# Two expert numbers taken early: the first head's two best experts computed straight from its top keys

## The chip, the cores and the metric

The kernel runs on one core of one Trainium2 chip. The metric is the device time of one execution in microseconds (us); lower is better. Its matrix products run on TensorE (PE in the profile, its weight loads PEld), element-wise work on VectorE (DVE), ScalarE (ACT) and GpSimd (POOL); SyncE (SP) issues most of the weight transfers, and POOL issues the indirect ones.

## The reference, cut to what matters

Two transformer blocks follow one another on 256 tokens of width 1024. The first ends in a layer of experts chosen per token (`peer_ffn`), and the change lies in it:

```
q = (xb @ w_query).reshape(tb, 8, 2, 128)
s = einsum('thpd,hpnd->thpn', q, sub_keys)            # 8 heads, 2 halves, 128 keys each
top_s, top_i = top_k(s, 16)                           # the 16 best keys of each half
cand_s = top_s[:, :, 0, :, None] + top_s[:, :, 1, None, :]
cand_i = top_i[:, :, 0, :, None] * 128 + top_i[:, :, 1, None, :]
best_s, pos = top_k(cand_s, 16)                       # the 16 best sums of the 256 pairs
eid = take_along_axis(cand_i, pos)                    # 16 expert numbers per head
gate = softmax(best_s)
act = gelu(einsum('thkd,td->thk', expert_down[eid], xb))
out = einsum('thkd,thk->td', expert_up[eid], gate * act)
```

An expert number is the key of the first half times 128, plus the key of the second half. `top_k` gives values in falling order, so the best pair of a head is always (best key of half 0, best key of half 1), and the second best pair is one of (best, second) and (second, best).

## The kernel before

The 256 tokens are two tiles of 128 (t = 0 and 1), a token on each partition. Each token has 8 heads x 16 slots = 128 experts, so that there are 256 fetches: one per tile and slot. A fetch (`fetch`, the indirect transfer at L764) reads for each of 128 tokens one row of 2048 floats of `uv` (the expert's down vector and its up vector side by side) into a buffer `uv`. It is issued by POOL, which first needs the expert numbers in `eid`. Each fetch is then used in four steps: VectorE multiplies the down half with the normed token `xn` and sums (`junk`, L768); ScalarE applies Gelu and the gate (L770, L771) and builds a diagonal matrix `dg` from the 128 weights (L773); TensorE multiplies `dg` with the up half and accumulates in PSUM (L775, two products of 512 columns, each shown as two instructions). The buffer is free again after the last of these. There are seven `uv` buffers at first (`uvs = [up] * 7`), and nine after the query weights are done and their memory is given back.

The expert numbers come from `queries` (the query projection, in pieces of weights that SP loads as `raw`, ScalarE rounds to `wh` at L178, VectorE turns into the remainder `wl` at L179, and TensorE multiplies three times at L184 to L186), the scores `sS` (L643, L644), `extract` (the 16 best of a row: the best eight at L607, their places at L610, their removal at L613, the next eight at L616, their places at L619) and `choose` (80 candidate sums, `extract` once more on these, and the look-up that ends in `eid` at L689 and the gates at L697). `picks` strings these together for a group of heads as a generator; `picking` takes steps from it, up to a credit of time or to the end of a group.

The order at the start of the stage, as the program is written: the query projection of the first two pieces and the scores of head 0 for both tiles; `picking(1e6, 0, 1)`, all of head 0's extraction and choice for tile 0; then, queued behind the write of `eid` on VectorE, the product of `xn` with the tokens (L800) and the next piece of `queries`; then the loop over the fetches of tile 0, in which after each slot come some steps of later heads' picks, and after every few slots one more piece of the query projection, each queued behind that slot's product on VectorE and its diagonal on ScalarE (`behind`). After the last query piece (slot 59) the loop goes on with pieces of the memory's key and value projection in the query's place. The second tile's 128 fetches follow, and then the second block.

The program is built by a layer that places the semaphores itself and fixes each engine's queue before the run: it takes instructions in the order in which they are written, and where one would still wait by its own cost figures, it may put a later one that is ready in front. So a small instruction can stand a little before or behind its place in the text.

Of the kernel before, what the change touches and what calls it, by code (L numbers as in the profile page):

```python
# [14 lines left out]
U32 = mybir.dt.uint32  # L15
AF = mybir.ActivationFunctionType
OP = mybir.AluOpType
# [108 lines left out]
class K:  # L126
# [573 lines left out]
    def experts(self):  # L700
# [3 lines left out]
        nc, I = self.nc, self.I  # L704
        with self.tc.tile_pool(name="p2", bufs=1, reuse_waits="tile") as p2, \
                self.tc.tile_pool(name="up", bufs=1, reuse_waits="tile") as up:
            def P(shape, tag, dt=F32, bufs=1):
                return p2.tile([128] + shape, dt, name=tag, tag=tag, bufs=bufs)
# [6 lines left out]
            sS = [[P([2, 128], f"sS{t}{h}") for h in range(8)] for t in range(2)]  # L715
            vals = [P([16, 16], f"vals{t}") for t in range(2)]
            idx = [P([16, 16], f"idx{t}", U32) for t in range(2)]
            self.gate = [P([8, 16], f"gate{t}") for t in range(2)]
            self.eid = [P([8, 16], f"eid{t}", U32) for t in range(2)]
            mr = [P([2, 128], f"mr{i}") for i in range(2)]  # L720
            xn = [P([1024], "xn0"), None]

            def picks(t, h0, H):
                for h in range(h0, h0 + H):
                    yield from self.extract([sS[t][h][:, i] for i in range(2)], [mr[h % 2][:, i] for i in range(2)],
                                            [vals[t][:, 2 * h + i] for i in range(2)],
                                            [idx[t][:, 2 * h + i] for i in range(2)], 410)
                yield from self.choose(t, h0, H, vals, idx, P)

            units = [(0, h, 1) for h in range(4)] + [(0, 4, 2), (0, 6, 2)] + [(1, h, 2) for h in (0, 2, 4, 6)]  # L730
            pick = [(u, picks(*u)) for u in units]
            debt = [0]

# [22 lines left out]
            def fetch(t, acc):  # L756

                gates = self.gate[t].rearrange("p h k -> p (h k)")
                eids = self.eid[t].rearrange("p h k -> p (h k)")
                for s in range(128):  # L760
                    pool = uvs[count[0] % len(uvs)]
                    count[0] += 1
                    x = pool.tile([128, 2048], F32, name="uv", tag="uv", bufs=uvs.count(pool))
                    nc.gpsimd.indirect_dma_start(x, None, I["uv"],  # L764
                                                 bass.IndirectOffsetOnAxis(ap=eids[:, s:s + 1], axis=0))
                    w = up.tile([128, 1], F32, name="dots", tag="dots", bufs=6)
                    junk = self.junk([128, 1024], "junk", BF)
                    self.dot = nc.vector.scalar_tensor_tensor(junk, x[:, :1024], 1.0, xn[t], op0=OP.mult, op1=OP.mult,  # L768
                                                              accum_out=w)
                    nc.scalar.activation(w, w, AF.Gelu, scale=self.r[:, t:t + 1])  # L770
                    nc.scalar.activation(w, w, AF.Copy, scale=gates[:, s:s + 1])  # L771
                    dg = up.tile([128, 128], F32, name="dg", tag="dg", bufs=4)
                    self.diag = nc.scalar.activation(dg, self.ident, AF.Copy, scale=w)  # L773
                    for d in range(2):
                        nc.tensor.matmul(acc[d], dg, x[:, 1024 + 512 * d:1536 + 512 * d], start=s == 0, stop=s == 127)  # L775
                    yield s
# [11 lines left out]
            with self.tc.tile_pool(name="qp", bufs=1, reuse_waits="tile") as qp:  # L788
                skT = qp.tile([128, 16, 128], F32, name="skT")
                nc.gpsimd.dma_start(skT[:, 0:4], I["skT"][:, 0:4])  # L790
                query = Filler(self.queries(qp, skT, sS))
                query(2)
                with self.tc.issue_after(self.raw.ins):
                    nc.sync.dma_start(xn[0], I["ffn_gr"].to_broadcast([128, 1024]))
                    nc.sync.dma_start(skT[:, 4:16], I["skT"][:, 4:16])
                query(1)
                n = 4
                picking(1e6, 0, 1)
                with self.tc.issue_after(self.chosen.ins):
                    nc.vector.tensor_mul(xn[0], xn[0], self.xr[:, 0])  # L800
                    query(1)
                acc = two()
                tile0 = fetch(0, acc)
                for s in tile0:
                    with behind():
                        if s in (3, 7, 11) or s > 11 and s % 6 == 5:
                            query(1)
                            n += 1
                        picking(750, 0, min(8, (n + 1) // 2))
                        if s in due:  # L810
                            picking(1e6, *due[s])
                    if n >= 15:
                        break
                query.rest()
            self.qraw_cm.__exit__(None, None, None)
            with self.tc.tile_pool(name="up2", bufs=1, reuse_waits="tile") as up2:
# [19 lines left out]
                for s in fetch(1, acc):  # L836
                    with behind():
                        if s in (4, 10):
                            self.joined(0, s // 10, acc0[s // 10], gg, nc.vector)
                        if s > 10:  # L840
                            picking(750, 1, 8)
                        if s in due:
                            picking(1e6, 1, due[s])
                        if s % 6 == 2 and 10 < s < 100:
                            self.memory(1)
                        if s == 100:
                            self.memory.rest()
                        if s == 112:
                            ws = [self.piece(I["w_latq"][k], [2, 432]) for k in range(3)]
                    if s == 120:  # L850
                        A = [self.pa([128, 512]) for _ in range(2)]
                        self.latents(ws, 0, A[0])
# [860 lines left out]
```

## Time and profile before

| what | value |
|---|---|
| median of 3 runs | 1310.26 us (1310.0 to 1311.74) |
| the profiled execution: its own time | 1309.71 us |
| its span in the trace | 1307.9 us |
| granted TensorE clock, mean | 0.987 of full speed |
| busy: PE, DVE, ACT, POOL | 89%, 72%, 55%, 24% of the span |
| moved by DMA | 388.63 MB, 297 GB/s over the span |
| of it by POOL's indirect fetches (queue q0) | 268.72 MB |

The shares are means over stages with different limits: the stage of the fetches runs from about 145 us to 840 us, and the second block fills the rest. Times in the trace are counted from the start of the span. The profiled execution took 1.8 us more than its span.

### The profile page before, as it was taken

Reading aid. Unit: us, or ns where it says so; the run is one execution under the profiler, and the core shown is the slowest. Engines: PE = TensorE matmul, PEld = TensorE weight load, DVE = VectorE, ACT = ScalarE, POOL = GpSimd, SP = SyncE. Lnnn points to the kernel's source line nnn. Section 1 sums busy time; section 2 is a strip of 40 time slices with the busy share of each in tenths; the row PEclk is TensorE's granted clock in tenths of the full one; section 3 lists DMA queues with packets and bytes.
Section 4 is the critical chain, followed back from the end, with each engine's and each line's share of the span. In section 5 each row is a group of like instructions: output and inputs, shape, how many; then the busy total and the mean of one; then the engine's idle time right before and its main releaser. Section 6 shows DMA issues by size and latency. Waiting matters only on the chain. (4 is left out here: it accounts for less than half of the span.)

```text
span 1307.9 us, 16937 instructions
## 1 busy us (share of the span) xinstructions
PE 1170.6 (89%) x5430; PEld 788.3 (60%) x5430; DVE 942.7 (72%) x2252; ACT 715.9 (55%) x1627; POOL 319.3 (24%) x274
## 2 busy tenths in 40 slices
PE   7999799998879888888887778799999999999996
PEld 5787554444324343344442223389987898999995
DVE  5878687675998886555554445588977886988887
ACT  6676456453555445543443444558787565655554
POOL 0000344454445444344443333110000000000001
PEclk9999899999999999999999999999999999999998
DMA  7835699999999999999999999355424464566562
GB/s 269 284 129 170 247 419 420 420 420 401 422 421 417 420 419 421 420 421 420 421 420 421 421 421 419 160 181 164 132 97 145 135 221 142 183 185 186 188 184 96
DMA packets 82203, 388.63 MB, mean 297 GB/s; under 512 B 8244, under 2 KB 10372, under 8 KB 49348
## 3 DMA queue, kind: packets, MB, share of 16 engines
q0 software_dynamic: 36976, 268.72, 49.5%
q1 hardware_dynamic: 43124, 116.22, 27.3%
q10 hardware_dynamic: 2016, 2.62, 0.5%
q8 instruction: 43, 0.70, 0.2%
q14 instruction: 44, 0.36, 0.1%
HBM read 384.38 MB, written 3.15 MB: 296 GB/s over the span
## 5 line engine op out<-in xcount | busy, mean ns | idle before, releaser
L775 PE MATMUL pb<-uv,dg 128*128 128x512 f32 x1024 | 496.1, 618 | 104.7 <-ACT dg L773 103.8
L768 DVE SCALAR_TENSOR_TENSOR junk<-uv,xn 128x1024 bf16<-128x1024 f32 x256 | 312.5, 1221 | 177.1 <-DMA uv<-in_uv_dram,eid 173.6
L775 PEld LDWEIGHTS pb<-uv,dg 128*128 128x128 f32 x1024 | 181.8, 192 | 389.5 <-ACT dg L773 247.4
L764 POOL DMA_INDIRECT uv<-in_uv_dram,eid x256 | 302.0, 1180 | 405.8 <-PE pb L775 245.4
L179 DVE TENSOR_TENSOR wl<-raw,wh 128x1024 fp32r<-128x1024 f32 (+3 forms) x203 | 246.9, 1220 | 104.6 <-ACT wh L178 103.4
L178 ACT ACTIVATE wh<-raw 128x1024 fp32r<-128x1024 f32 (+3 forms) x203 | 211.1, 1044 | 149.3 <-PE pa L186 32.3
L770 ACT ACTIVATE dots<-dots,rs_y 128x1 f32<-128x1 f32 x256 | 75.2, 294 | 336.1 <-DVE junk L768 335.5
L185 PE MATMUL pb<-nTl,wh 128*128 128x256 f32 x416 | 117.9, 284 | 0.0
L184 PE MATMUL pb<-nTh,wh 128*128 128x256 f32 x416 | 117.7, 283 | 0.0
L186 PE MATMUL pb<-nTh,wl 128*128 128x256 f32 x416 | 117.5, 283 | 0.0
L773 ACT ACTIVATE dg<-cvt,dots 128x128 f32<-128x128 f32 x256 | 102.7, 401 | 14.0 <-DVE memkv L944 6.2
L1564 POOL TENSOR_TENSOR xs<-xr,ng 128x512 f32<-128x512 f32 x4 | 5.0, 1280 | 313.2 <-DVE xr L1562 313.2
L185 PEld LDWEIGHTS pb<-nTl,wh 128*128 128x128 f32 x416 | 79.6, 192 | 0.8
L184 PEld LDWEIGHTS pb<-nTh,wh 128*128 128x128 f32 x416 | 79.6, 192 | 0.8
L771 ACT ACTIVATE dots<-dots,gate 128x1 f32<-128x1 f32 x256 | 75.3, 294 | 8.5 <-ACT dots L770 0.4
L186 PEld LDWEIGHTS pb<-nTh,wl 128*128 128x128 f32 x416 | 79.6, 192 | 0.0
L184 PE MATMUL pa<-nTh,wh 128*128 128x256 f32 x256 | 79.1, 309 | 0.0
L186 PE MATMUL pa<-nTh,wl 128*128 128x256 f32 x256 | 74.2, 290 | 5.3 <-DVE wl L179 5.3
L185 PE MATMUL pa<-nTl,wh 128*128 128x256 f32 x256 | 72.9, 285 | 0.0
L184 PE MATMUL pa<-wh,nTh 128*128 128x512 f32 (+1 forms) x144 | 58.1, 412 | 8.6 <-ACT wh L178 8.0
L185 PE MATMUL pa<-wl,nTh 128*128 128x512 f32 (+1 forms) x144 | 57.5, 400 | 2.4 <-DVE wl L179 2.4
L186 PE MATMUL pa<-wh,nTl 128*128 128x512 f32 (+1 forms) x144 | 56.6, 393 | 0.0
(458 smaller groups left out, 1885.1 us busy)
## 6 DMA issues: line engine op xcount, KB each, us to landing
raw<-in_w_ffn_up_dram SPq DMA_DIRECT2D x44, 512.0 KB, 3.7
raw<-in_w_out_dram SPq DMA_DIRECT2D x24, 512.0 KB, 3.7
raw<-in_w_in_dram SPq DMA_DIRECT2D x23, 512.0 KB, 4.5
raw<-in_w_ffn_down_dram SPq DMA_DIRECT2D x22, 512.0 KB, 3.6
raw<-in_w_query_dram SPq DMA_DIRECT2D x16, 512.0 KB, 7.0
raw<-in_w_xbc_dram SPq DMA_DIRECT2D x16, 512.0 KB, 4.0
raw<-in_w_mem_v_dram SPq DMA_DIRECT2D x8, 512.0 KB, 10.3
uv<-in_uv_dram,eid POOLq DMA_INDIRECT x256, 17.6
```

What stands on the lines that cost most here:

```text
L178: nc.scalar.activation(h[:, s], raw[:, s], AF.Copy)
L179: self.wl = nc.vector.tensor_sub(lo[:, s], raw[:, s], h[:, s])
L184: mm(out, a[0], b[0], start=start, stop=False)
L185: mm(out, a[0], b[1], start=False, stop=False)
L186: mm(out, a[1], b[0], start=False, stop=stop)
L764: nc.gpsimd.indirect_dma_start(x, None, I["uv"], bass.IndirectOffsetOnAxis(ap=eids[:, s:s + 1], axis=0))
L768: self.dot = nc.vector.scalar_tensor_tensor(junk, x[:, :1024], 1.0, xn[t], op0=OP.mult, op1=OP.mult, accum_out=w)
L770: nc.scalar.activation(w, w, AF.Gelu, scale=self.r[:, t:t + 1])
L771: nc.scalar.activation(w, w, AF.Copy, scale=gates[:, s:s + 1])
L773: self.diag = nc.scalar.activation(dg, self.ident, AF.Copy, scale=w)
L775: nc.tensor.matmul(acc[d], dg, x[:, 1024 + 512 * d:1536 + 512 * d], start=s == 0, stop=s == 127)
L1564: nc.gpsimd.tensor_mul(xs[:, c], xr[:, t, c], g[:, c])
```

## The change

In the extraction of tile 0's head 0, after its second step (the best eight keys of both halves and their places are known) a new function `firsts` is called. With nine VectorE instructions on one or two columns it computes the head's two best expert numbers into a tile of their own, `first`: the best is the pair of the two best keys; for the second it compares the sum (best, second) with (second, best). The rest of the extraction and the whole choice stay as they are and still write all 16 numbers to `eid`. The fetches of slots 0 and 1 of tile 0 read their expert numbers from `first` and no longer from `eid`. Nothing else is edited.

```diff
@@ -720,11 +720,33 @@
+            first = P([2], "first", U32)
+
+            def firsts():
+                v, ix = vals[0], idx[0]
+                nc.vector.scalar_tensor_tensor(first[:, 0:1], ix[:, 0, 0:1], 128.0, ix[:, 1, 0:1],
+                                               op0=OP.mult, op1=OP.add)
+                s, d, f = P([2], "firsts"), P([2], "firstd"), P([2, 2], "firstf")
+                nc.vector.tensor_copy(f, ix[:, 0:2, 0:2])
+                nc.vector.tensor_add(s[:, 0:1], v[:, 0, 0:1], v[:, 1, 1:2])
+                nc.vector.scalar_tensor_tensor(s[:, 1:2], v[:, 0, 1:2], v[:, 1, 0:1], s[:, 0:1],
+                                               op0=OP.add, op1=OP.is_gt)
+                nc.vector.tensor_scalar(s[:, 0:1], s[:, 1:2], -1.0, 1.0, op0=OP.mult, op1=OP.add)
+                nc.vector.tensor_sub(d, f[:, :, 1], f[:, :, 0])
+                nc.vector.scalar_tensor_tensor(d[:, 0:1], d[:, 0:1], s[:, 1:2], f[:, 0, 0:1], op0=OP.mult, op1=OP.add)
+                nc.vector.scalar_tensor_tensor(d[:, 1:2], d[:, 1:2], s[:, 0:1], f[:, 1, 0:1], op0=OP.mult, op1=OP.add)
+                nc.vector.scalar_tensor_tensor(first[:, 1:2], d[:, 0:1], 128.0, d[:, 1:2], op0=OP.mult, op1=OP.add)
+
             def picks(t, h0, H):
                 for h in range(h0, h0 + H):
-                    yield from self.extract(...)
+                    for n, cost in enumerate(self.extract(...)):
+                        if (t, h, n) == (0, 0, 1):
+                            firsts()
+                        yield cost
@@ -762,7 +784,8 @@
-                                                 bass.IndirectOffsetOnAxis(ap=eids[:, s:s + 1], axis=0))
+                                                 bass.IndirectOffsetOnAxis(
+                                                     ap=(first if t == 0 and s < 2 else eids)[:, s:s + 1], axis=0))
```

## Rows read from the trace of the kernel before

**Rows 1.** The page's span in 40 slices: DMA share in tenths, GB/s moved.
```profile
DMA  7835699999999999999999999355424464566562
GB/s 269 284 129 170 247 419 420 420 420 401 422 421 417 420 419 421 420 421 420 421 420 421 421 421 419 160 181 164 132 97 145 135 221 142 183 185 186 188 184 96
```

**Rows 2.** Stretches of 2 us: length, PE, PEld, DVE, ACT, POOL busy, clock, DMA share, GB/s.
```profile
138.00:140.00 2.00, 2.00 (x19) 2.00 (x18) 1.89 (x15) 1.03 (x2) 0.00 (x0) 1.00 0.01 4
...
144.00:146.00 2.00, 0.00 (x0) 0.00 (x0) 2.00 (x3) 0.00 (x0) 0.98 (x1) 0.50 0.00 0
146.00:148.00 2.00, 1.54 (x7) 1.54 (x8) 0.40 (x1) 0.00 (x0) 1.39 (x3) 0.50 0.57 123
148.00:150.00 2.00, 2.00 (x11) 2.00 (x11) 0.00 (x0) 0.00 (x0) 1.63 (x2) 0.50 0.95 391
```

**Rows 3.** A stretch of 20 us, the same columns.
```profile
160.00:180.00 20.00, 17.78 (x78) 10.59 (x77) 16.97 (x59) 11.69 (x28) 8.64 (x7) 1.00 1.01 419
```

**Rows 4.** Timeline of VectorE, head 0's picks: start, length, instruction.
```profile
136.26 0.28 DVE L610 FIND_INDEX8 idx<-vals,sS 128x8 uint32<-128x128 f32 x1
...
140.40 0.17 DVE L671 SCALAR_TENSOR_TENSOR ru<-rf 128x16 f32<-128x16 f32 x1
140.49 0.17 DVE L672 SCALAR_TENSOR_TENSOR ru<-rf 128x16 f32<-128x16 f32 x1
140.69 0.19 DVE L673 TENSOR_TENSOR rab<-rg,ru 128x32 f16<-128x32 f32 x1
...
143.96 0.17 DVE L689 SCALAR_TENSOR_TENSOR eid<-rij 128x16 uint32<-128x16 f32 x1
...
145.19 1.22 DVE L179 TENSOR_TENSOR wl<-raw,wh 128x1024 fp32r<-128x1024 f32 x1
```

**Rows 5.** Timeline of POOL: the fetches' issue; in brackets idle before, releaser.
```profile
145.02 1.15 POOL L764 DMA_INDIRECT uv<-in_uv_dram,eid  x1 [34.29 <-DVE eid L689]
146.47 0.97 POOL L764 DMA_INDIRECT uv<-in_uv_dram,eid  x1 [0.30 <-issue]
...
157.41 1.76 POOL L764 DMA_INDIRECT uv<-in_uv_dram,eid  x1 [3.18 <-PE pb L775]
...
182.69 1.87 POOL L764 DMA_INDIRECT uv<-in_uv_dram,eid  x1 [4.39 <-DVE best L607]
...
315.16 1.68 POOL L764 DMA_INDIRECT uv<-in_uv_dram,eid  x1 [5.29 <-DVE wl L179]
```

**Rows 6.** Timeline of VectorE: products with fetched rows, slots 0, 3, 4, 16, last two.
```profile
150.95 1.23 DVE L768 SCALAR_TENSOR_TENSOR junk<-uv,xn 128x1024 bf16<-128x1024 f32 x1 [4.55 <-DMA uv<-in_uv_dram,eid]
...
159.68 1.23 DVE L768 SCALAR_TENSOR_TENSOR junk<-uv,xn 128x1024 bf16<-128x1024 f32 x1 [0.51 <-DMA uv<-in_uv_dram,eid]
...
164.12 1.22 DVE L768 SCALAR_TENSOR_TENSOR junk<-uv,xn 128x1024 bf16<-128x1024 f32 x1
...
196.79 1.23 DVE L768 SCALAR_TENSOR_TENSOR junk<-uv,xn 128x1024 bf16<-128x1024 f32 x1 [0.20 <-DMA uv<-in_uv_dram,eid]
...
834.95 1.22 DVE L768 SCALAR_TENSOR_TENSOR junk<-uv,xn 128x1024 bf16<-128x1024 f32 x1 [1.25 <-DMA uv<-in_uv_dram,eid]
837.43 1.23 DVE L768 SCALAR_TENSOR_TENSOR junk<-uv,xn 128x1024 bf16<-128x1024 f32 x1 [1.25 <-DMA uv<-in_uv_dram,eid]
```

**Rows 7.** Instructions on tile junk: what VectorE waited for (us, times).
```profile
  DMA uv<-in_uv_dram,eid: 173.6, 120
```

**Rows 8.** Timeline of TensorE at the start of the fetches.
```profile
146.46 0.58 PE L186 MATMUL pa<-nTh,wl 128*128 128x256 f32 x1 [5.28 <-DVE wl L179]
...
153.46 5.54 PE L775 MATMUL pb<-uv,dg 128*128 128x512 f32 x8 [2.48 <-ACT dg L773]
...
162.06 1.98 PE L775 MATMUL pb<-uv,dg 128*128 128x512 f32 x4 [0.57 <-ACT dg L773]
```

**Rows 9.** Stretches of 2 us where the query's memory is given back, columns of Rows 2.
```profile
316.00:318.00 2.00, 2.00 (x17) 1.88 (x16) 0.95 (x8) 1.11 (x4) 1.70 (x2) 1.00 0.92 328
318.00:320.00 2.00, 2.00 (x8) 0.82 (x6) 0.00 (x0) 1.11 (x3) 1.39 (x3) 1.00 0.90 340
```

More of the change, by code (lines that the diff above doesn't have):

```diff
@@ L721, in experts @@
             xn = [P([1024], "xn0"), None]
+            first = P([2], "first", U32)
[13 more added lines that the diff above has]
+                nc.vector.scalar_tensor_tensor(first[:, 1:2], d[:, 0:1], 128.0, d[:, 1:2], op0=OP.mult, op1=OP.add)
             def picks(t, h0, H):
                 for h in range(h0, h0 + H):
-                    yield from self.extract([sS[t][h][:, i] for i in range(2)], [mr[h % 2][:, i] for i in range(2)],
-                                            [vals[t][:, 2 * h + i] for i in range(2)],
-                                            [idx[t][:, 2 * h + i] for i in range(2)], 410)
+                    for n, cost in enumerate(self.extract(
+                            [sS[t][h][:, i] for i in range(2)], [mr[h % 2][:, i] for i in range(2)],
+                            [vals[t][:, 2 * h + i] for i in range(2)], [idx[t][:, 2 * h + i] for i in range(2)], 410)):
+                        if (t, h, n) == (0, 0, 1):
+                            firsts()
+                        yield cost
                 yield from self.choose(t, h0, H, vals, idx, P)
```

## The prediction, written before the run

> **What bounds the kernel now.** Start with the span in slices [rows 1]. From the sixth slice to the twenty-fifth (about 163 to 817 us) the DMA row is all nines and the rate stands at 419 to 422 GB/s in nearly every slice. No other stage looks like that: before it the rate is 129 to 284, after it below 225. So half of the kernel is a transfer stage at a steady rate, and in such a stage time is bytes over rate. One fetch is 128 rows of 8 KB, 1.05 MB: at 420 GB/s 2.50 us. The products with fetched rows agree: at the end of the stage they start 2.48 us apart, each after a wait of 1.25 us for its DMA [rows 6], and over the stage 120 of 256 products waited for a fetch, 173.6 us in all [rows 7].
>
> Then look at where the stage begins [rows 2]. From 138 to 146 us the DMA engines move next to nothing (0.01 to 0.00 of their time, four stretches), then 0.57, then 0.95 and full from there on. VectorE is full in the empty stretch (1.89 and 2.00 of 2.00): it runs head 0's extraction and choice. POOL stands until the numbers are there: its first fetch starts at 145.02 after 34.29 us of idling, released by `eid` [rows 5], which VectorE wrote from 143.96 to 144.13 [rows 4], so 0.89 us from the end of the write to the issue. The DMA engines have 1.1 us of work (0.57 of 2.00) in 146 to 148, so data begin to flow at about 146.9, 1.9 us after the issue.
>
> The chain is therefore: scores of head 0, picks on VectorE, first fetch, then bytes at 420 GB/s to the last fetch, whose product starts at 837.43 [rows 6], and behind it the second block. What moves the end of the bytes moves the whole rest.
>
> **What the change adds.** Nine small VectorE instructions between the places of the best eight (done at 136.54, [rows 4]) and the first removal. The trace has neighbours of that kind: L671 and L672, independent, start 0.09 us apart although each lasts 0.17; L673, which needs L672's result, starts 0.20 after it [rows 4]. Four of the nine need the result of the one just before (the comparison, its complement, the first blended key, the last sum), five do not: 4 x 0.20 + 5 x 0.09 = 1.25 us. Bounds: 9 x 0.09 = 0.8 if the planner fills the waits with removals that are ready, 9 x 0.20 = 1.8 if every one waits. I take 1.1, between the written order and the filled one. VectorE has no gap there [rows 2], so `eid`, and with it the third fetch, `xn` and the next weight split (at 145.19) come 1.1 us later. Waiting behind that split are TensorE's query products at 146.46, which stood 5.28 us for it [rows 8]; they now stand about 6.4.
>
> A rule speaks for a higher price. The Trainium skill, VectorE: DVE Perf Modes, section "The DRAIN you can't avoid", says that the next operation does not start until the pipe is empty, except where it is not held. By that each of the nine would cost its whole length; the same page's section "The TRN2 errata" gives (N+151)/0.96 ns for a float addition, an estimate of 0.16 us each, 1.4 us in all and a gain 0.3 us smaller than mine. The trace shows starts 0.09 us apart, so here it is the exception that holds for independent ones [rows 4].
>
> **What the change moves.** The issue of fetches 0 and 1, and their 2 x 2.50 us of data. `first` is complete 1.3 us after 136.54 in written order, at about 137.9; with four removals or searches of 0.28 us (the length in [rows 4]) put between, 138.9. Then 0.89 us to the issue: fetch 0 starts between 138.8 and 139.8, fetch 1 1.45 later (145.02 to 146.47, [rows 5]). Data flow from 140.7 at the earliest or 141.7 at the latest, for 5.0 us: done by 145.7 or 146.7. The third fetch is issued at 145.02 + 1.1 = 146.1 and its data start at 148.0. So both fetches fit whole into the empty stretch, with at least 1.3 us to spare; a slower issue (1.87 us is one of the long ones, [rows 5]) would still fit. Credit: 5.0 us of transfer leaves the saturated stage. No transfer is added and no queue of SP's is passed.
>
> The Trainium skill, DMA: Bandwidth & Descriptors, section "Where 436 GB/s comes from", says that from HBM the limit is about 358 GB/s. By that a fetch would take 2.93 us and the credit would be an estimated 5.9. The trace moves 419 to 422 for hundreds of us [rows 1], so the measurement decides.
>
> **The sum.** The saturated stage starts 1.1 us later and holds 5.0 us less: -3.9 us. On the profiled execution: 1309.71 - 3.9 = 1305.8. The median of the runs is 0.55 above that execution, so the forecast is 1310.26 - 3.9 = **1306.4 us**.
>
> What is late next? The first products need `xn`, at about 146.5 in place of 145.3, and then find slots 0 and 1 landed. Slots 2 and 3 land 3.9 us earlier than now. TensorE: its query products run from 147.6 to about 152.1, then slots 0 and 1 follow at once, where now it idles 2.48 us and then takes 5.54 us for eight instructions [rows 8] at a clock that had fallen to 0.50 [rows 2]; four take 1.98 us a little later [rows 8]. So it should be done with slot 1 at about 156.1 and no longer at 159.0. The eighth fetch, which waits for slot 0's buffer (157.41, [rows 5]), can go some 2 us earlier, while six are queued in front.
>
> **Rivals.**
> *Compute holds the first stretch.* Product 4 starts at 164.12 without a wait for data, and so do all twelve from slot 4 to 15; slot 16 waits only 0.20 [rows 6]. VectorE is busy 16.97 and TensorE 17.78 of 20 us there [rows 3]. If that work keeps today's times or comes 1.1 us later, buffers come free no earlier, and DMA could run dry. The place is 182.69, where POOL waited 4.39 us for a buffer [rows 5]. Up to there 15 fetches and about three query pieces of half a fetch were issued: 15 x 2.5 + 3 x 1.25 = 41.2 us of data from 146.9, enough to 188.1; the next flows 1.9 after its issue, at 184.6. The reserve is 3.5 us. With data 3.9 us ahead and buffers 1.1 late, 1.5 us are lost: gain 2.4, time 1307.9. Against it: slots 0 to 3 all waited for data (4.55 us the first, 0.51 the last, [rows 6]), so the chain of products should move with them.
>
> *The fetches don't start early*, because POOL is held by something else than `first`, or both wait for `eid` after all. Then only the nine instructions count: 1311.4. Rows 5 show no other reason for the 34 us of idling.
>
> *Slower: the hand-over of the query's memory.* At 315.16 POOL waits 5.29 us for the last query piece's split [rows 5], because two new buffers lie in that piece's memory; the queue empties, and DMA falls to 328 and 340 GB/s [rows 9], 0.8 us lost in 4. VectorE's queue there is fixed by the planner from its own times, which the change shifts. Each product that it puts in front of that split costs one spacing of data, 2.5 us; two of them eat the gain (3.9), three make it 1310.26 - 3.9 + 7.5 = 1313.9. Against it: the loop that orders them is not edited, and the products there hang on the data's times, so they should move together.
>
> **How the numbers follow.** 0.2% of the time, 2.6 us, is about what a measurement of this kernel can tell from no change. Forecast 0.68; compute holds 0.20; not early 0.06; hand-over 0.06. The forecast's own range: the nine at 0.8 or 1.8 us give 1306.1 and 1307.1; the 0.8 us lost at the hand-over may vanish or double: 1305.3 to 1307.9. Of its 0.68, 0.64 lie more than 2.6 us below the median. Of the compute rival 0.02 do too; its other 0.18 and the case of no early start make "same" 0.28 with the forecast's 0.04. The hand-over gives "slower" 0.06. The range takes in the forecast, half a microsecond below it for the spread of the runs, and the compute rival up to nearly no gain: 1304.8 to 1309.8; it leaves out the last two cases.
>
> **What would show it.** In the changed kernel's trace: two fetches on POOL between 138.5 and 141.5, released by `first`; the third about 1.1 us later than today's first; DMA share near 1 for some 5 us in the stretch 140 to 147; the third slot's product at about 152.0 (issue 146.1 plus the 5.9 us that slot 0 took from issue to product), slot 3's at 155.8 (159.68 - 3.9, [rows 6]); rate 420 up to the end, and the last product at 833.5. Everything after it moves by the same amount. The prediction is wrong if the last product moves by much less than the third one (then DMA ran dry between, and the windows show where), if the second block takes another length than today's (1307.9 - 837.4 = 470.5 us), or if the nine take more than 2 us.

## The result, and the profile after

The changed kernel is faster, and by more than forecast. Its median is 1302.97 us (1300.8 to 1306.56, four runs) beside 1310.66 us for the kernel before: a ratio of 0.9950, 95% interval 0.9938 to 0.9963. Repeated later (e1_after below) it took 1303.17 us beside 1310.26: 0.9942 (0.9928 to 0.9955), so 7 to 8 us less. The forecast was 3.9 us less, 1306.4 us with a range from 1304.8 to 1309.8; the measured median lies below that range. The profiled execution shown here is the slowest of its four (1306.56 us, span 1304.7). Of this, 1.8 us come from its second block, which took 472.3 us; in the repeat it took 470.5, as before.

The page's span in 40 slices, kernel after: DMA share in tenths and GB/s.

```profile
DMA  8834799999999999999999999445424464655662
GB/s 268 286 130 155 304 419 419 421 419 386 425 423 418 422 421 422 423 421 422 423 422 422 424 423 420 158 161 162 130 95 145 141 218 145 180 190 182 189 182 96
```

Against [rows 1] two things differ. The fifth slice, in which the fetches begin, moves 304 GB/s in place of 247: data flow earlier. And from the eleventh slice on the rate is 1 to 3 GB/s higher in all fetch slices but one, which nothing in the forecast accounts for.

Stretches of 2 us at the start of the fetches, kernel after; columns as in [rows 2].

```profile
138.00:140.00 2.00, 2.00 (x19) 2.00 (x18) 2.00 (x16) 1.51 (x2) 1.20 (x2) 1.00 0.03 10
140.00:142.00 2.00, 1.52 (x13) 1.32 (x12) 1.83 (x16) 0.49 (x2) 0.80 (x1) 1.00 0.84 250
142.00:144.00 2.00, 0.56 (x4) 0.36 (x4) 1.86 (x12) 1.61 (x3) 0.00 (x0) 1.00 1.08 385
144.00:146.00 2.00, 0.00 (x0) 0.00 (x0) 1.83 (x7) 0.51 (x1) 0.09 (x1) 1.00 0.85 352
146.00:148.00 2.00, 0.04 (x1) 0.04 (x1) 2.00 (x3) 0.00 (x0) 1.70 (x2) 0.58 0.15 61
148.00:150.00 2.00, 2.00 (x9) 2.00 (x10) 2.00 (x9) 0.59 (x2) 1.85 (x1) 0.50 0.83 238
```

The stretch that was empty holds the two fetches: the shares from 140 to 148 add up to 2.92 of 4 stretches, 5.8 us of DMA work for 2.1 MB, the bytes of two fetches, and it ends before the third fetch's data come.

Timeline of VectorE, kernel after: the new instructions among the removals, then `eid` and four of the products.

```profile
136.95 0.28 DVE L610 FIND_INDEX8 idx<-vals,sS 128x8 uint32<-128x128 f32 x1
137.15 0.14 DVE L733 TENSOR_TENSOR firsts<-vals 128x1 f32<-128x1 f32 x1
137.21 0.08 DVE L613 MATCH_VALUE_LOAD mr<-vals,sS 128x8 f32 x1
137.28 0.28 DVE L613 MATCH_REPLACE8 mr<-vals,sS 128x128 f32<-128x128 f32 x1
137.47 0.15 DVE L729 SCALAR_TENSOR_TENSOR first<-idx 128x1 uint32<-128x1 uint32 x1
137.53 0.16 DVE L732 CAST firstf<-idx 128x4 f32<-128x4 uint32 x1
...
138.59 0.14 DVE L740 SCALAR_TENSOR_TENSOR first<-firstd 128x1 uint32<-128x1 f32 x1
...
145.46 0.17 DVE L689 SCALAR_TENSOR_TENSOR eid<-rij 128x16 uint32<-128x16 f32 x1
...
147.82 1.22 DVE L791 SCALAR_TENSOR_TENSOR junk<-uv,xn 128x1024 bf16<-128x1024 f32 x1
...
156.11 1.23 DVE L791 SCALAR_TENSOR_TENSOR junk<-uv,xn 128x1024 bf16<-128x1024 f32 x1 [1.78 <-DMA uv<-in_uv_dram,eid]
160.55 1.22 DVE L791 SCALAR_TENSOR_TENSOR junk<-uv,xn 128x1024 bf16<-128x1024 f32 x1
...
832.44 1.22 DVE L791 SCALAR_TENSOR_TENSOR junk<-uv,xn 128x1024 bf16<-128x1024 f32 x1 [1.24 <-DMA uv<-in_uv_dram,eid]
```

The planner put removals between the nine, and starts stand 0.06 apart where neighbours are independent (137.47, 137.53). Slot 0's product starts at 147.82 (150.95 in [rows 6]), slot 3's at 156.11 (159.68), slot 4's at 160.55 (164.12), the last at 832.44 (837.43): 3.1 to 3.6 us earlier at the start of the stage and 5.0 at its end. These are times from the start of the span; head 0's picks began 0.7 us later in this execution than in the one before (below).

Timeline of POOL, kernel after: first three fetches, the eighth, two later ones with long waits.

```profile
138.50 1.03 POOL L786 DMA_INDIRECT uv<-in_uv_dram,first  x1 [26.88 <-DVE firstd L739]
139.83 0.97 POOL L786 DMA_INDIRECT uv<-in_uv_dram,first  x1 [0.30 <-DVE rix L675]
145.91 1.68 POOL L786 DMA_INDIRECT uv<-in_uv_dram,eid  x1 [5.11 <-DVE eid L689]
...
155.13 0.94 POOL L786 DMA_INDIRECT uv<-in_uv_dram,eid  x1 [0.74 <-PE pb L798]
...
179.22 1.99 POOL L786 DMA_INDIRECT uv<-in_uv_dram,eid  x1 [4.39 <-DVE best L607]
...
311.94 1.68 POOL L786 DMA_INDIRECT uv<-in_uv_dram,eid  x1 [2.76 <-DVE wl L179]
```

The two are issued at the early end of the window that was named (138.5 to 141.5), the third only 0.89 later than the first was [rows 5], and the wait at the hand-over is 2.76 us in place of 5.29.

### The profile page after: what moved, and what is told of

The parts are those of the page before. It is cut to its first block, busy times and chain, and to the rows that moved or that the text cites. A ratio compares the mean times of both kernels' runs of the same rounds, so it can differ in the third digit from the quotient of the medians.

```text
span 1304.7 us, 16946 instructions
## 1 busy us (share of the span) xinstructions
PE 1171.1 (90%) x5430; PEld 788.5 (60%) x5430; DVE 943.8 (72%) x2261; ACT 715.7 (55%) x1627; POOL 314.5 (24%) x274
## 4 chain that ended last, share of the span: by engine, by line
PE 39%; DMA 34%; DVE 13%; ACT 6%; issue 5%; POOL 1%; SPq 0%; POOLq 0%; DVEq 0%; ACTq 0%
DMA uv<-in_uv_dram,eid 32%; PE pa L184 5%; PE pa L185 5%; PE pa L186 5%; DVE junk L791 5%; PE pb L184 4%; PE pb L185 4%; PE pb L186 4%; PE pa L1563 4%; PE pb L798 2%; DMA raw<-in_w_in_dram 2%; DVE wl L179 2%; ACT wh L178 2%; POOL uv L786 1%; ACT dg L796 1%
## 5 line engine op out<-in xcount | busy, mean ns | idle before, releaser
L786 POOL DMA_INDIRECT uv<-in_uv_dram,eid x254 | 295.1, 1162 | 380.1 <-PE pb L798 253.8
```

Of the source, the lines that this page charges most:

```text
L786: nc.gpsimd.indirect_dma_start(x, None, I["uv"], bass.IndirectOffsetOnAxis(ap=(first if t == 0 and s < 2 else eids)[:, s:s + 1], axis=0))
```

## How the stage is measured below

The profiled executions reach head 0's picks at times that differ by up to 1.4 us (the first MAX8, which finds the best eight, starts at 134.86 to 136.22), so the stage is counted from that MAX8, and in two pieces: up to the product of slot 16, where the early fetches should show, and from the product of slot 59 to the last product, where only the rate should. Each number, in us, is the difference of two starts in the timeline of VectorE, where the first MAX8 of the kernel before and of the changed kernel are:

```profile
135.53 0.49 DVE L607 MAX8 vals<-sS 128x8 f32<-128x128 f32 x2 [1.08 <-ACT sS L644]
...
136.22 0.49 DVE L607 MAX8 vals<-sS 128x8 f32<-128x128 f32 x2 [1.07 <-ACT sS L644]
```

The third column is where the fetch buffers begin in a partition, worked out from the built programs and given modulo 512 bytes: the seven early buffers / the two that come with the query's memory.

| kernel | early fetches | buffers mod 512 | MAX8 to slot 16 | slot 59 to last | ratio to before (95%) |
|---|---|---|---|---|---|
| before | 0 | 192 / 384 | 61.26 | 527.07 | |
| e1_before | 0 | 192 / 384 | 61.47 | 527.44 | 0.9999 (0.9990 to 1.0008) |
| after | 2 | 320 / 0 | 57.16 | 525.30 | 0.9950 (0.9938 to 0.9963) |
| e1_after | 2 | 320 / 0 | 57.02 | 525.46 | 0.9942 (0.9928 to 0.9955) |
| e1_ops | 0 | 320 / 0 | 62.22 | 524.99 | 0.9985 (0.9976 to 0.9994) |
| e1_one | 1 | 224 / 416 | 59.18 | 528.37 | 0.9989 (0.9980 to 0.9998) |
| e2_same | 2 | 192 / 384 | 57.86 | 527.22 | 0.9969 (0.9959 to 0.9980) |
| e2_pad128 | 0 | 320 / 0 | 62.00 | 524.76 | 0.9973 (0.9963 to 0.9984) |
| e2_pad320 | 0 | 0 / 192 | 61.94 | 520.55 | 0.9933 (0.9919 to 0.9946) |
| e2_early4 | 4 | 320 / 0 | 55.26 | 524.73 | 0.9923 (0.9908 to 0.9939) |
| e3_all512 | 0 | 0 / 0 | 62.25 | 519.60 | 0.9928 (0.9912 to 0.9945) |
| e3_all256 | 0 | 256 / 256 | 61.83 | 520.32 | 0.9927 (0.9911 to 0.9944) |
| e3_best | 2 | 0 / 0 | 56.61 | 519.95 | 0.9900 (0.9883 to 0.9916) |
| e3_pad32 | 0 | 224 / 416 | 61.56 | 528.31 | 1.0012 (1.0003 to 1.0022) |

The first piece varies by 1.0 us among kernels without early fetches (61.26 to 62.25), the second by 0.4 between two executions of one kernel.

## Experiments

**The change taken apart: both kernels again, the nine instructions alone, and one early fetch.** The first two repeat the kernels unchanged on one chip.

> The changed kernel once more, beside the kernel before on one chip. Theory A (credit and price: two fetches of 2.5 us leave the saturated stage, nine small VectorE instructions cost 0.8 us): 4.2 us less than before, and the steady rate in the stage as before. Theory B (the change also lifts the steady rate or shortens what follows): 6 to 8 us less again, with a rate of 423 GB/s where before has 420.5. Theory C (runs differ by some us whatever the kernel): the gain moves between 3 and 8 us from run to run, and before shows a like spread.

> The kernel before against itself, for the spread and for the steady rate of another execution. Theory A: 0 within 1 us, last product at 837.4 after the same start, rate 420.5. Theory C: a difference of 2 us or more between executions of one and the same program, and a rate between 420 and 424 in 340 to 800 us.

The difference stands: 1303.17 us beside 1310.26, and 1310.33 for the kernel before run against itself.

e1_ops computes all nine but lets every fetch read `eid`:

```diff
-    ap=(first if t == 0 and s < 2 else eids)[:, s:s + 1], axis=0))
+    ap=eids[:, s:s + 1], axis=0))
```

> The nine instructions alone: they are computed, but all fetches read their expert numbers from eid as before. Theory A: 0.8 us slower than before (the price alone), eid written 0.8 us later. Theory B: if the order or the place of things in memory, and not the early transfers, gives the further gain, it is faster than before by 2 to 4 us. If each of the nine costs its whole length: 1.4 us slower.

It took 1308.39 us, 1.9 below before, although it only adds work. The price of the nine is there: from the first MAX8 to the end of the write of `eid` 9.41 us in place of 8.60, so 0.81 us. But the second piece is 2.1 us shorter than before's (524.99 beside 527.07), with no fetch moved. So a part of the gain does not come from the early fetches. The first piece, beside it, shows the credit alone: after and e1_ops differ only in what two fetches read, and 57.16 is 5.1 us less than 62.22.

e1_one computes only the first expert number, with one instruction, and fetches only slot 0 early; of the four new tiles only `first` is left:

```diff
             def firsts():
                 ...
                 nc.vector.scalar_tensor_tensor(first[:, 0:1], ...)
-                s, d, f = P([2], "firsts"), P([2], "firstd"), P([2, 2], "firstf")
-                ...
-    ap=(first if t == 0 and s < 2 else eids)[:, s:s + 1], axis=0))
+    ap=(first if t == 0 and s < 1 else eids)[:, s:s + 1], axis=0))
```

> Only slot 0 is taken early, its number made with one instruction; slot 1 reads eid. Theory A: 2.5 - 0.1 = 2.4 us less than before. Theory B (an extra that comes with any early start): more than 4 us less. No gain if the empty stretch can't be used.

The first piece is 2.1 us shorter than before's, about half of the 4.1 that the change brings there. The second is 1.3 us longer, and the whole only 1.4 us faster (1308.81), where 2.4 were expected. What sets the second piece follows neither the early fetches nor the added instructions. What else these three kernels change is memory: each small tile takes 32 bytes of a partition in a pool that lies below the fetch buffers, so the buffers begin 128 bytes further on in the changed kernel and in e1_ops, and 32 in e1_one.

**The memory apart from the change.** e2_same is the whole change, with the four small tiles laid into words of `iota` that nothing uses, so that every fetch buffer begins where it did before:

```diff
-            first = P([2], "first", U32)
+            first = iota[:, 0:2].bitcast(U32)
-                s, d, f = P([2], "firsts"), P([2], "firstd"), P([2, 2], "firstf")
+                s, d, f = iota[:, 2:4], iota[:, 4:6], iota[:, 6:10].rearrange("p (a b) -> p a b", b=2)
```

> The whole change, but its four small tiles lie in the unused words of the tile iota, so that every fetch buffer keeps the address that it has in the kernel before. Theory X (the addresses of the fetch buffers set the steady rate; the change moved them by 128 bytes per partition): slot 59's product to the last one takes 527.2 us as before, and the gain is credit less price alone, 4.2 us. Theory Y (the nine instructions or the order of the queues give the extra): 525.3 us, and the gain is 6 to 7 us as in the changed kernel.

e2_pad128 is the kernel before with `iota` made 128 bytes longer and nothing else; e2_pad320 makes it 320 bytes longer (a tile of 96 words):

```diff
-            iota = P([16], "iota")
+            iota = P([48], "iota")[:, :16]
```

> The kernel before with the tile iota made 128 bytes longer, so that the fetch buffers lie where the changed kernel has them; no instruction is added. Theory X: slot 59's product to the last one takes 525.2 us where before takes 527.2, and the kernel is 2 us faster. Theory Y: 527.2 and no gain.

> The kernel before with the tile iota made 320 bytes longer: the first seven fetch buffers then start at a multiple of 512 bytes, the two later ones 192 bytes behind one. Theory X, if what counts is a start at a multiple of 512: seven of nine buffers gain where the changed kernel has two of nine, so slot 59's product to the last one takes 520 us and the kernel is 7 us faster. Theory X, if only the distance from a multiple of 64 counts: 527 us as before. Theory Y: 527 us.

Timeline of VectorE, products of slot 59 and of the last slot, first e2_same, then e2_pad128.

```profile
305.55 1.22 DVE L791 SCALAR_TENSOR_TENSOR junk<-uv,xn 128x1024 bf16<-128x1024 f32 x1 [1.26 <-DMA uv<-in_uv_dram,eid]
...
832.77 1.22 DVE L791 SCALAR_TENSOR_TENSOR junk<-uv,xn 128x1024 bf16<-128x1024 f32 x1 [1.24 <-DMA uv<-in_uv_dram,eid]
```

```profile
310.38 1.23 DVE L768 SCALAR_TENSOR_TENSOR junk<-uv,xn 128x1024 bf16<-128x1024 f32 x1 [1.25 <-DMA uv<-in_uv_dram,eid]
...
835.14 1.22 DVE L768 SCALAR_TENSOR_TENSOR junk<-uv,xn 128x1024 bf16<-128x1024 f32 x1 [1.24 <-DMA uv<-in_uv_dram,eid]
```

They part the two effects cleanly. e2_same reaches slot 59 earlier (170.47 us after the first MAX8, before 174.83: 4.4 less) and then takes 527.2 us like the kernel before. e2_pad128 reaches slot 59 at 174.91, like before, and then takes 524.8 like the changed one. By the ratios, e2_same is worth 0.31% (4.1 us) and e2_pad128 0.27% (3.5 us); together 7.6, and the whole change in the repeat 0.58%, 7.6 us. That the sums agree to a tenth is luck: each of the three is uncertain by 1.4 us or more, and by the second pieces of the profiled executions e2_pad128 gains only 2.3. e2_pad320, again without one instruction more, is 8.5 us faster than before: with the seven early buffers at multiples of 512 bytes the second piece takes 520.6 us.

**Is there room for more early fetches?** e2_early4 also lets slots 2 and 3 be fetched early. It has no third and fourth number to fetch, so these slots fetch the experts of slots 0 and 1 again: that part of the computation is another one, and the bytes are the same.

```diff
-    ap=(first if t == 0 and s < 2 else eids)[:, s:s + 1], axis=0))
+    ap=(first[:, s % 2:s % 2 + 1] if t == 0 and s < 4 else eids[:, s:s + 1]), axis=0))
```

> The changed kernel with four fetches early: slots 2 and 3 of tile 0 read the numbers of slots 0 and 1 again, so four slots fetch only two experts (a change of what is computed). Theory A: the credit is what is left of the empty stretch, so that the gain over the changed kernel is some 2.3 us (0.30 and 1.70 of 2.00 us unused in its 144 to 148 us, and a part of the next), not 5.0. If every early fetch were worth its 2.5 us: 5.0 us.

1300.22 us: 1.8 to 1.9 us less than the two executions of the changed kernel in the first piece, and 2.8 to 2.9 in the medians, where two more whole fetches would be 5.0. After two fetches the empty stretch has little left: of the stretches above from 140 us on, 146 to 148 is the only one with DMA mostly idle.

**How far the buffers' place goes.** e3_all512 is the kernel before with the small tiles `dots` taken out of the pool of the buffers and `iota` 128 bytes longer, so that all nine buffers begin at multiples of 512 bytes; e3_all256 makes `iota` 384 bytes longer instead, and all nine begin 256 behind such a multiple.

```diff
-            iota = P([16], "iota")
+            iota = P([48], "iota")[:, :16]
-                    w = up.tile([128, 1], F32, name="dots", tag="dots", bufs=6)
+                    w = P([1], "dots", bufs=6)
```

> The kernel before with all nine fetch buffers at a multiple of 512 bytes: the six small tiles dots are moved out of the pool of the buffers and the tile iota is made 128 bytes longer; no instruction is added. Theory X (the start of a buffer counts, each buffer for itself): two of nine aligned were worth 2.1 us from slot 59's product to the last one, seven 6.7, so nine give 8.8: 518.4 us, and with the 2.6 us that the seven gained ahead of slot 59 the kernel is 11 us faster. If the gain of the seven came from something else that 320 bytes moved: less than 7 us.

> The kernel before with all nine fetch buffers 256 bytes behind a multiple of 512 (iota 384 bytes longer, dots moved as in the last run). Theory X with a step of 512: no gain, 527 us from slot 59's product to the last. Theory X with a step of 256: 518.4 us and 11 us faster, as with 512.

Both are 0.72 to 0.73% faster than before, 1301.17 and 1300.69 us: multiples of 256 do as well as multiples of 512. The second piece takes 519.6 and 520.3 us, a little more than the 518.4 that e2_pad128 and e2_pad320 had led to expect, and the gain is 9 us and not 11; with e2_pad320 (two buffers at 192) already at 520.6, the two late buffers' own share is within the spread.

e3_pad32 is the kernel before with `iota` 32 bytes longer, so the addresses of e1_one without its early fetch.

```diff
-            iota = P([16], "iota")
+            iota = P([24], "iota")[:, :16]
```

> The kernel before with iota 32 bytes longer: the fetch buffers lie where the kernel with one early fetch has them, 32 bytes off a multiple of 64. Theory X: slot 59's product to the last one takes 528.4 us as there (before 527.2), and the kernel is 1 us slower. If it was that kernel's order of work: 527.2.

1311.34 us, 0.12% slower (0.03 to 0.22), and the second piece is e1_one's, 528.3. So a shift can also cost.

e3_best is the changed kernel with only the line of `dots` moved as above; the new tiles' 128 bytes then do what the longer `iota` did.

> The changed kernel with dots moved out of the pool of the fetch buffers, which puts all nine at a multiple of 512 bytes. Theory X and theory A together: credit less price (4.2) plus the aligned buffers (11) is 15 us faster than before, about 1295 us. If a faster stage runs into TensorE or VectorE instead (TensorE busy 17 to 19 of 20 us between 160 and 320 us): 10 to 13 us.

1296.94 us (1296.39 to 1297.02) beside 1309.87: 0.9900, the fastest of all, and some 6 us below the changed kernel. Expected were 15 us and 12.9 came. That lies in the range expected if TensorE or VectorE held the faster stage. But e3_best reaches slot 59 4.4 us before e3_all512 does (168.02 and 172.38 us after the first MAX8), the whole of credit less price; what was too high is the 11 us for the aligned buffers, which brought 8.7 in e3_all512.

Stretch of 700 to 800 us, columns as in [rows 2], last one GB/s: before, e3_pad32, e2_same, after, e2_pad128, e3_best, one fence each.

```profile
700.00:800.00 100.00, 79.50 (x165) 27.72 (x165) 49.53 (x81) 41.07 (x120) 37.55 (x40) 1.00 1.01 421
```

```profile
700.00:800.00 100.00, 78.75 (x160) 27.09 (x160) 48.48 (x79) 40.48 (x121) 37.93 (x40) 1.00 1.01 420
```

```profile
700.00:800.00 100.00, 79.92 (x174) 29.47 (x173) 52.24 (x83) 41.05 (x120) 36.34 (x39) 1.00 1.01 421
```

```profile
700.00:800.00 100.00, 80.35 (x174) 29.78 (x175) 52.24 (x83) 41.14 (x121) 36.75 (x39) 1.00 1.01 423
```

```profile
700.00:800.00 100.00, 80.24 (x172) 29.47 (x173) 50.94 (x81) 40.19 (x118) 38.21 (x40) 1.00 1.01 423
```

```profile
700.00:800.00 100.00, 81.39 (x177) 30.65 (x178) 51.05 (x83) 42.04 (x123) 39.92 (x40) 1.00 1.01 426
```

In all six the DMA share is full and no compute engine is, so the stage is bound by the transfers each time; only the last column moves, and it moves with the buffers' addresses: 421 and 421 at before's, 423 and 423 at after's, 420 with 32 bytes more, 426 at multiples of 512. The lengths agree: 527.07 / 519.95 is 1.014, and 426 / 421 is 1.012.

The records of the single DMA packets in the traces show that it is the fetched rows that take longer. In the second piece a row of 8 KB took exactly 309 ns in 99% of the packets or more in e3_all512, e3_all256 and e3_best, and in 98% in e2_pad320. In after and e2_pad128 46% took 309 ns, in before and e2_same 22 to 23%, in e3_pad32 and e1_one 18%; most of the others took 311 to 321. The mean is 310.0 ns in e3_best, 312.9 in after, 314.2 in before and 314.9 in e3_pad32, and 314.2 / 310.0 is 1.014 again. The buffers do not count one by one, as the expectation of e3_all512 had assumed: in e2_pad320 the two late buffers, which take 44 of the 197 fetches of the second piece, begin 192 bytes behind a multiple of 512, and yet only 1.6% of all its rows took another time than 309 ns.

The shift moves VectorE's tiles and not only the buffers, but these do not explain it: by the built programs, `junk` begins at 64 modulo 512 in after, e1_one, e3_pad32 and e3_best alike, whose second pieces take 525.3, 528.4, 528.3 and 519.95 us. The weights' buffers (`raw`, `wh`, `wl`) begin at the same places modulo 512 in all programs.

## Why the prediction was right and wrong

**The bound, right.** A transfer stage at a steady rate, in which bytes that leave it are time saved. Forecast were 2.5 us for each early fetch, less the price. One early fetch brought 2.1 us of the first piece beside before, and 2.4 beside e3_pad32, which has its addresses. Two brought 3.4 (e2_same beside before), 4.1 (after beside before) or 4.8 (after beside e2_pad128, which has its addresses); kernels without early fetches differ by up to 1.0 there, so this is no finer than that.

**The price, a little high.** Taken was 1.1 us, the bounds were 0.8 and 1.8; measured are 0.81 (8.60 to 9.41 us, the same in e1_ops), the low end: the planner filled the waits with removals. The Trainium skill, VectorE: DVE Perf Modes, section "The DRAIN you can't avoid", lets an operation start only when the pipe is empty, except where it is not held. Without the exception the prediction made of this an estimated 1.4 us, nearly twice what was measured, so the trace, with starts 0.06 us apart of operations that last 0.15, agrees with the exception.

**The place of the early fetches, right.** Issues at 138.50 and 139.83 lie in the window 138.5 to 141.5; the third slot's product came at 152.28 (forecast 152.0), slot 3's at 156.11 (155.8), the eighth fetch 2.3 us earlier (some 2). TensorE went from its query products to the slots without idling, as forecast, at 152.82 (152.1). Two things are a little off. The working had put the first issue at 138.8 or later, 0.89 us after both numbers; it came 0.88 us after its own number alone (137.47 + 0.15), before the second was written (138.59 + 0.14). And the near agreement of the absolute times is in part luck, since head 0's picks began 0.7 us later in this execution than in the trace forecast from (136.22 and 135.53). The third fetch was issued 0.28 us after `eid` was written (145.63 to 145.91), where before it took 0.89; that gave back some of the price and was not foreseen.

**The sum for the mechanism, right.** -3.9 us were forecast; e2_same, which is the change with the buffers where they were, gives 4.4 up to slot 59 and 4.1 by its ratio.

**The step that failed: "rate 420 up to the end".** The sum held one term for the bytes and one for the start, and took the rate of [rows 1] for a constant of the stage. The list of what the change adds names nine instructions and leaves out the four small tiles they write. Those tiles move every fetch buffer by 128 bytes, and with that the rate goes from 421 to 423 GB/s: 1.8 us over 525 in the profiled executions (2.0 in the repeat), 3.5 us (2.1 to 4.8) by the ratio of e2_pad128. This is what took the time below the range: 1302.97 with 1.8 to 3.5 us added is 1304.8 to 1306.5, from the range's lower end to the forecast. The sign stated for it, the last product at 833.5, would have shown it: it came at 832.44, although head 0's picks began 0.7 us later than in the trace of before.

**The rivals.** Compute did not hold the first stretch: from slot 16 to slot 59 it took 113.76 us (before 113.57), and POOL's long wait for a buffer came 3.5 us earlier (179.22, in [rows 5] 182.69) at the same 4.39 us. The fetches did start early. The hand-over lost no 2.5 us: its wait got shorter, and e2_same, with the change's order of work, needs 527.2 us from slot 59 on, as before.

**The second block.** The prediction named another length of the second block as a sign of being wrong, and in the profiled executions of after, e1_one, e2_pad320, e3_all512 and e3_all256 it is 1.4 to 1.8 us longer (471.9 to 472.3 us; 470.5 in the others). e1_after is the same program as after and took 470.5, so it is no property of the change. Beside the repeat, the difference arises some 25 us behind the last product. From 20 to 24 us behind it TensorE is busy for 1.8 us in all fourteen traces, and DMA moves nothing. Then, in these five traces and in no other, the granted clock stood at the lower of its two levels, 1.2 GHz, for a while, in after from 856.28 to 859.70, and the products of 512 columns started 0.43 us apart in place of 0.23. First after, then e1_after, columns as in [rows 2]:

```profile
856.00:858.00 2.00, 2.00 (x6) 1.59 (x6) 2.00 (x5) 1.27 (x2) 0.00 (x0) 0.57 0.61 154
```

```profile
856.00:858.00 2.00, 2.00 (x11) 1.58 (x10) 2.00 (x4) 0.53 (x2) 0.00 (x0) 1.00 0.66 207
```

**What stays open.** Why the rate depends on the address, and why two of nine buffers off a multiple of 256 cost next to nothing where nine cost 7 us. And why the clock fell in some executions behind the last product and not in others.

## What to carry to other kernels

In a stage that the transfers hold, costing an edit means listing its tiles as well as its instructions: ask where the buffers behind them in memory begin afterwards, and keep the places fixed when the edit itself is to be measured, as e2_same does. Before working on the order of such a stage, try the buffers at multiples of 256 bytes: it cost no instruction and was worth 9 us here, more than the change that was studied. Early work for a stretch in which the transfers stand idle pays whole fetches only until that stretch is full.

## What the runs showed of the hardware that was not expected

The rate of the indirect fetches (rows of 8 KB, one per partition) depends on where the buffers, taken together, begin in a partition. From slot 59 to the last product: 528.3 us with buffers at 224 / 416 modulo 512, 527.1 at 192 / 384, 524.8 to 525.5 at 320 / 0, 520.6 at 0 / 192, 519.6 to 520.3 where all begin at a multiple of 256. In the last case nearly every row of 8 KB took 309 ns, at 192 / 384 314.2 on average.

The Trainium skill, DMA: Bandwidth & Descriptors, section "How a descriptor splits into AXI transactions", says that a read that does not begin at a multiple of 256 bytes fetches the bytes from the boundary below it for nothing. The runs here moved the end that is written. If the same held there, the nine buffers would carry on average 210, 178, 50, 43 and 0 such bytes per 8 KB in the order of the paragraph above, an estimated 2.6, 2.2, 0.6, 0.5 and 0%; measured against 519.6 us are 1.7, 1.4, 1.0 to 1.1, 0.2 and up to 0.1%. The order is the same, the sizes are not, and an average over single buffers does not fit e2_pad320's packets, so this is a resemblance and no explanation that was shown.
